# Silu gates in pairs with the attention outputs multiplied in, sums of x by need, squares moved, and two gate tiles ahead of the stick-breaking stage

## The chip, the cores and the metric

The kernel runs on one core of a Trainium2 chip. The metric is the device time of one execution in microseconds (us); the time of a kernel is the median of its runs. The profile is one further execution, recorded by the hardware profiler; its time and its span stand in the table below.

## What is computed

One decoder layer with two attention branches that read the same normalised input, over 16 meta tokens and 2048 real tokens, width 1024, all in float32:

```python
xn = rms_norm(h, norm_gain)                 # h = [pad, 16 meta tokens, x]
proj = xn @ w_in                            # 6400 columns, split into:
sb_q, sb_k, sb_v, sw_q, sw_k, sw_v, sb_z, sw_z, g_sb, g_sw = split(proj)
o_sb = stick_breaking_attention(sb_q, sb_k, sb_v)       # 8 heads of 64, all earlier tokens
o_sw = sliding_window_sink_attention(rope(sw_q), rope(sw_k), sw_v)   # 16 heads, window 128
y_sb = (o_sb * silu(sb_z)) @ w_branch_sb
y_sw = (o_sw * silu(sw_z)) @ w_branch_swa
merged = sigmoid(g_sb) * y_sb + sigmoid(g_sw) * y_sw
out = rms_norm(h + merged @ w_out, final_norm_gain)
```

A stick-breaking weight is exp(log_sigmoid(z) + the sum over the later keys of log_sigmoid(-z)). The change concerns the gates: `sb_z` (4 column tiles of 128, called SBZ), `sw_z` (8, SWZ), `g_sb` (8, GSB) and `g_sw` (8, GSW), 28 column tiles of `proj` in all.

## The kernel before

**Tiling.** The tokens lie in reverse in 4 groups of 512. A column tile is 128 columns of `w_in` for one group: the product of a 1024 x 128 weight tile with the group's 1024 x 512 normalised x. Each float32 operand is split into a high and a low part (`xh`, `xl`; `wh`, `wl`), and a product is high by high, high by low and low by high: 3 matmuls of 128x128 by 128x512 for each of 8 slices of 128, so 24 to a column tile (lines 412 to 414). The splitting of a raw weight is a cast on ScalarE (ACT) and a subtraction on VectorE (DVE), or both on GpSimd in some stages; the split weights are written to DRAM (`h_in_w_in`, `l_in_w_in`) the first time, and loaded from there in the second half.

**Stages.** The groups are done in two halves, [2, 3] and then [0, 1]. A half has a sliding-window stage, then a stick-breaking stage (function `stick`), into which gate column tiles are woven so that TensorE (PE) has work while the scans of the stick run on DVE, then the gate **pairs**, then two last gate tiles. After half 0 stands `prep`, which normalises the x of the next half (its row sums of squares are needed for that). After half 1 stands `finish`, the two branch projections, the merge and the output projection. One gate tile (`gts[1:2]`) stands alone ahead of each stick stage; `REST` (12 and 18) says how many gate tiles are done before the pairs; two single column tiles open the pairs stage.

**A pair** is two gate column tiles for both groups of the half, done with seven half-size products in place of eight (functions `pair_weights`, `seven`, `gate_pair`): sums and differences of the weights (`s`, `s4`), made on DVE, meet sums and differences of x (`t1` to `t4`), made once per half by `sums_of_x`. A product is 12 matmuls. PE takes them in the order 11·11, s2·t2, 12·21, s1·t1, s3·t3, 22·t4, then the next pair's 11·11, then s4·22. The first pair comes while `t1` to `t4` are still being made. For each k of 4, `sums_of_x` makes x11, x12, x22 whole (line 598), then differences (609 to 611), the splits of t2, t3, t1 (603, 604), then t4 (616).

**Squares.** The sums of squares for the next half's x are made inside the stick stage of half 0: 16 tiles `xq` are loaded (in a ring of two, shared with the tiles `q2` of the stick's queries) and squared on ACT with an accumulated sum (line 1004). The reciprocal root stands between the stick stage and the pairs.

**Gated outputs.** Silu gates are written to DRAM (`zs`, `zw`), attention outputs too (`od` of the stick, `ow` of the window). `gated` (line 197) later loads a tile of each, multiplies them on DVE (line 202) and splits the product (204, 206) for the branch projections: `od, zs` inside `finish`, `ow, zw` beside the last two gate tiles.

**What sets the order.** PE's order is that of the code, by hand (`manual_schedule`). The other engines' order is made by a scheduler, and each engine runs its list in order. All DMAs are issued by SyncE (SP) through one helper (lines 55 to 58), in order: a DMA that waits holds those behind it. Buffers are rings: `xs` (4 buffers, function `ring_x`), `tmp` (7), `wh` and `wl` (3 each), `raw` (2).

## Time and profile before

| | before |
|---|---|
| time, median of 3 runs | 2176.36 us (2169.45 to 2180.69) |
| the profiled execution: time, span | 2171.38 us, 2169.7 us |
| granted TensorE clock, mean of the span | 0.988 |
| PE busy | 2106.6 us (97%) |
| DVE, ACT, GpSimd busy | 1497.0 (69%), 1072.5 (49%), 246.9 us (11%) |
| DMA | 389.82 MB, 180 GB/s over the span |
| PE idle for a load of the stick's queries (`q<-qd`) | 8.5 us in 2 waits |
| ACT idle for the tiles `xq` | 20.6 us in 11 waits |
| loads of `gated`: `tmp<-ow`, `tmp<-zw` beside the last tiles; `a<-od`, `a<-zs`, `a<-ow`, `a<-zw` in `finish` | 16 of 256 KB each |

The stages in the span (us): stick of half 0 from about 375 to 610, pairs of half 0 from 610, the last gate tiles and `prep` around 780, the second half's stick from 1140 to 1620, its pairs from 1620, the last tiles with `gated` from about 1700, then `finish`. PE is busy nearly throughout, so what a change can win is PE's idle stretches and the lower clock that follows them. A window of the profile lists, for a stretch, each engine's busy time with its count of instructions, the clock granted to PE (1.00 is full) and the DMA engines' busy share.

### The profile page before, as it was taken

To read this page: it belongs to the slowest core of one execution; us is meant where nothing else is said; L and a number is where in the kernel's file an instruction comes from. 1 tells how busy PE (TensorE), PEld (TensorE's weight loads), DVE (VectorE), ACT (ScalarE), POOL (GpSimd) and SP (SyncE) were. 2 spreads that over 40 slices of the span, in tenths; PEclk is the share of its full clock that TensorE was granted. 3 is DMA by queue.
4 is the path that set the end of the run, shared out by engine and by line. 5 is a ranking of instruction groups with operands and counts; after the bars stand their busy time and mean duration, and the time that the engine had idled before them with its cause. 6 is when DMAs were issued, how large, how long until landed. Compare 5 with 4: busy or idle time off the path is not lost.

```text
span 2169.7 us, 29865 instructions
## 1 busy us (share of the span) xinstructions
PE 2106.6 (97%) x10426; PEld 1744.1 (80%) x10426; DVE 1497.0 (69%) x2350; ACT 1072.5 (49%) x2541; POOL 246.9 (11%) x303
## 2 busy tenths in 40 slices
PE   8999999999989999999989999999999899999998
PEld 6788887778868878888878888888887688887887
DVE  7897885777785543877748888888884455554453
ACT  6677774556653234777745666666651211321131
POOL 2122334112000100122210000000000132000000
PEclk9999999999999999999999999999999899999999
DMA  9855546756436864544364333344235895558432
GB/s 335 302 175 176 193 146 203 227 177 199 163 112 222 297 215 157 164 154 148 136 195 124 110 122 117 117 120 124 72 106 197 302 356 184 196 200 299 148 118 78
DMA packets 178838, 389.82 MB, mean 180 GB/s; under 512 B 23200, under 2 KB 41440, under 8 KB 178688
## 3 DMA queue, kind: packets, MB, share of 16 engines
q1 hardware_dynamic: 178688, 387.92, 52.9%
q8 instruction: 82, 1.34, 0.3%
q14 instruction: 68, 0.56, 0.1%
HBM read 242.07 MB, written 145.70 MB: 179 GB/s over the span
## 4 chain that ended last, share of the span: by engine, by line
PE 79%; DVE 9%; DMA 6%; ACT 3%; issue 2%; SPq 1%; DVEq 0%; ACTq 0%
PE ps_g L412 10%; PE ps_g L413 10%; PE ps_g L414 10%; PE ps_z L1020 5%; PE ps_o L1076 5%; PE ps_t L1045 5%; PE ps_o L907 2%; PE ps_z L861 2%; PE ps_t L674 2%; PE ps_g L674 2%; PE ps_z L674 2%; DMA xq<-in_x 1%; PE ps_z L234 1%; PE ps_z L235 1%; PE ps_z L236 1%
## 5 line engine op out<-in xcount | busy, mean ns | idle before, releaser
L412 PE MATMUL ps_g<-xh,wh 128*128 128x512 f32 x1224 | 505.0, 413 | 10.0 <-ACT xh L1128 7.0
L413 PE MATMUL ps_g<-xl,wh 128*128 128x512 f32 x1224 | 482.6, 394 | 0.2
L414 PE MATMUL ps_g<-xh,wl 128*128 128x512 f32 x1224 | 481.9, 394 | 0.0
L414 PEld LDWEIGHTS ps_g<-xh,wl 128*128 128x128 f32 x1224 | 231.3, 189 | 52.3 <-DVE wl L112 0.4
L412 PEld LDWEIGHTS ps_g<-xh,wh 128*128 128x128 f32 x1224 | 232.4, 190 | 47.7 <-ACT xh L1128 7.0
L413 PEld LDWEIGHTS ps_g<-xl,wh 128*128 128x128 f32 x1224 | 232.7, 190 | 37.2 <-DVE xl L1129 1.3
L1023 ACT ACTIVATE row<-ps_z 128x512 f32<-128x512 f32 (+2 forms) x320 | 165.3, 516 | 141.9 <-PE ps_z L1020 129.3
L1032 DVE TENSOR_TENSOR_SCAN row<-row 128x528 f32<-128x528 f32 (+1 forms) x192 | 216.0, 1126 | 26.8 <-ACT row L1023 22.9
L116 DVE SCALAR_TENSOR_TENSOR wtl<-ps_t,wth 128x512 fp32r<-128x512 f32 (+1 forms) x320 | 189.7, 593 | 26.2 <-ACT wth L115 25.3
L1030 DVE TENSOR_TENSOR_SCAN row<-row,mask 128x512 f32<-128x512 f32 (+4 forms) x128 | 147.5, 1153 | 67.5 <-ACT row L1023 66.4
L115 ACT ACTIVATE wth<-ps_t 128x512 fp32r<-128x512 f32 (+1 forms) x320 | 170.5, 533 | 47.4 <-PE ps_t L1045 45.7
L1020 PE MATMUL ps_z<-kt,q 128*128 128x512 f32 (+4 forms) x640 | 181.4, 359 | 8.5 <-DMA q<-qd 8.5
L1045 PE MATMUL ps_t<-ident,row 128*128 128x128 f32 x1088 | 171.9, 273 | 8.6 <-DVE wtl L116 4.5
L1045 PEld LDWEIGHTS ps_t<-ident,row 128*128 128x128 f32 x1088 | 134.3, 140 | 44.8 <-DVE wtl L116 8.5
L111 POOL TENSOR_SCALAR wh<-raw 128x1024 fp32r<-128x1024 f32 (+1 forms) x49 | 52.3, 1067 | 1016.0 <-PE ps_o L674 558.8
L1020 PEld LDWEIGHTS ps_z<-kt,q 128*128 128x128 f32 x640 | 118.1, 190 | 30.6 <-issue 9.5
L1076 PE MATMUL ps_o<-wth,vc 128*128 128x512 f32 (+1 forms) x320 | 129.9, 406 | 1.7 <-ACT tmp L1080 1.7
L869 ACT ACTIVATE sc<-sc,nm 128x129 f32<-128x129 f32 x256 | 100.0, 393 | 40.9 <-DVE nm L867 40.1
L1076 PE MATMUL ps_o<-wtl,vc 128*128 128x512 f32 (+1 forms) x320 | 116.9, 365 | 0.2
L273 ACT CAST ringl<-gt 128x512 fp32r<-128x512 f32 x32 | 19.9, 622 | 137.2 <-DVE gt L271 134.4
L861 PEld LDWEIGHTS ps_z<-kk,q 128*128 128x128 f32 x512 | 69.7, 190 | 6.6 <-DVE q L842 0.7
L299 ACT ACTIVATE sq<-res 128x512 bf16<-128x512 f32 x32 | 20.2, 632 | 108.8 <-DVE res L295 108.7
(398 smaller groups left out, 4182.7 us busy)
## 6 DMA issues: line engine op xcount, KB each, us to landing
wh<-h_in_w_in SPq DMA_DIRECT2D x60, 512.0 KB
wl<-l_in_w_in SPq DMA_DIRECT2D x60, 512.0 KB
raw<-in_w_in SPq DMA_DIRECT2D x50, 512.0 KB
h_in_w_in<-wh SPq DMA_DIRECT2D x41, 512.0 KB
l_in_w_in<-wl SPq DMA_DIRECT2D x41, 512.0 KB
q<-qd SPq DMA_DIRECT2D x128, 128.0 KB
vc<-vd SPq DMA_DIRECT2D x48, 256.0 KB
kd<-tmp SPq DMA_DIRECT2D x32, 256.0 KB
```

Of the source, the lines that this page charges most:

```text
L115: A.activation(h, acc, AF.Copy, scale=scale)
L116: V.scalar_tensor_tensor(l, acc, scale, f32(h), op0=ALU.mult, op1=ALU.subtract)
L412: T.matmul(acc, lhsT=wh[:, k, :], rhs=xh[g][:, k, :], start=k == 0, stop=False)
L413: T.matmul(acc, lhsT=wh[:, k, :], rhs=xl[g][:, k, :], start=False, stop=False)
L414: T.matmul(acc, lhsT=wl[:, k, :], rhs=xh[g][:, k, :], start=False, stop=k == KT - 1)
L674: T.matmul(acc, lhsT=l[:, k, :], rhs=r[:, k, :], start=first and k == i == 0, stop=k == KT // 2 - 1 and i == 2, skip_group_check=not (firs ...
L1020: T.matmul(acc[:, :b - a], lhsT=lq, rhs=kt[h][:, k0 + a:k0 + b], start=t == 0, stop=t == 1)
L1023: A.activation(r[:, a:b], acc[:, :b - a], AF.Sigmoid, scale=-1.0)
L1030: V.tensor_tensor_scan(r[:, :w], r[:, :w], mask[0][:, :w], 1.0, op0=ALU.mult, op1=ALU.max)
L1032: V.tensor_tensor_scan(r[:, :w], r[:, :w], r[:, :w], last[j], op0=ALU.mult, op1=ALU.min)
L1045: T.transpose(tr[:, j * P:(j + 1) * P], rows_of[h, g, n - (j > i), j][:, k0:k0 + P], ident)
L1076: T.matmul(o[:, :n], lhsT=v, rhs=r, start=first and r is wh, stop=last and r is wl)
```

## The change

1. **Order of the gates.** There is now one order per half. Half 0 has 14 plain sigmoid gates first (GSB 0 to 7, GSW 0 to 5), then the 12 silu gates (SWZ 0 to 7, SBZ 0 to 3) as its six pairs, then the last two GSW. Half 1 has 12 plain ones, SWZ 0 to 5, two plain ones, and three pairs of SWZ 6, 7 and SBZ 0 to 3.
2. **Outputs multiplied in the pairs of half 0.** There each silu gate's tile is multiplied by its attention output (`times`: a load of `ow` or `od` into an `xs` buffer and a DVE multiplication, line 730 of the changed kernel). `gated` then loads one tile and multiplies nothing for the groups of half 0 (its second argument is `None`); for half 1 it is as before.
3. **Sums of x by need.** `sums_of_x` makes t2, t1 and t3 for all k, holding t1 in PSUM banks and t3 in the four `xs` buffers, then splits t1 and t3, then makes t4 from x21 less both parts of t2 (13 DVE instructions a k where there were 12). In the first pair (`lead`) the product 12·21 comes right after 11·11 in a bank of its own, and one DVE addition joins them.
4. **Squares among the pairs.** The 16 loads of x and Squares for the next half leave the stick stage and stand, four each, behind pairs 0 to 3 of half 0, in `xs` buffers; the reciprocal root stands behind pair 4.
5. **Two gate tiles ahead** of each stick stage instead of one (`gts[1:3]`), so one fewer is woven in.
6. **End of half 0.** The scale rows are made right after the pairs; both last tiles of group 2 come before `prep` and both of group 3 after it (before, one of group 3 stood ahead of it).

The number of PE matmuls for gates and pairs is the same. The diff, with repeated context left out:

```diff
         for k, g in keys:
-            a, b = stg(), stg()
+            a = stg()
             DMA(a, src[k][g])
-            DMA(b, zz[k][g])
-            V.tensor_tensor(a, a, b, op=ALU.mult)
+            if zz is not None:
+                b = stg()
+                DMA(b, zz[k][g])
+                V.tensor_tensor(a, a, b, op=ALU.mult)
...
-                    osb = gated(od, zs, [(k, g) for g in groups for k in range(4)], lambda: ringr(1), lambda: small("a", AB))
+                    osb = gated(*((zs, None) if half == 0 else (od, zs)), [(k, g) for g in groups for k in range(4)], lambda: ringr(1), lambda: small("a", AB))
...
-        for k in range(KT // 2):
-            yield q
+        ks = range(KT // 2)
+        held = [], []
+        for k in ks:
             b11, b12, b22 = (whole(n, k) for n in ("11", "12", "22"))
-            V.tensor_tensor(b11, b12, b11, op=ALU.subtract)
-            V.tensor_tensor(b12, b22, b12, op=ALU.subtract)
-            V.tensor_tensor(b22, b22, b11, op=ALU.subtract)
-            halves_of("t2", k, b22)
-            halves_of("t3", k, b12)
-            halves_of("t1", k, b11)
-            b21 = whole("21", k)
-            V.tensor_tensor(b21, b21, b22, op=ALU.subtract)
-            halves_of("t4", k, b21)
+            t3, t1 = ring_x(), ps(("t", "t", "o", "zm")[k])
+            V.tensor_tensor(t3, b22, b12, op=ALU.subtract)
+            V.tensor_tensor(b22, t3, b11, op=ALU.add)
+            parted("t2", k, b22)
+            V.tensor_tensor(t1, b12, b11, op=ALU.subtract)
+            held[0].append(t1)
+            held[1].append(t3)
+        yield q
+        for n, ts in zip(("t1", "t3"), held):
+            for k in ks:
+                parted(n, k, ts[k])
+        for k in ks:
+            b21, (t2h, t2l) = whole("21", k), (f32(t[:, k, :]) for t in q["t2"])
+            V.tensor_tensor(b21, b21, t2h, op=ALU.subtract)
+            V.tensor_tensor(b21, b21, t2l, op=ALU.subtract)
+            parted("t4", k, b21)
         yield q
...
-        product(a0, "11", "11", True, False)
+        product(a0, "11", "11", True, lead)
         A.copy(p1, a0)
+        if lead:
+            a3 = ps(tag)
+            product(a3, "12", "21", True, True)
+            t = tmp()
+            V.tensor_tensor(t, a3, p1, op=ALU.add)
+            use(0, 0, t)
         yield
...
-        product(a0, "12", "21", False, True)
-        use(0, 0, a0)
+        if not lead:
+            product(a0, "12", "21", False, True)
+            use(0, 0, a0)
+        a3 = ps(tag)
...
             if silu:
                 V.tensor_tensor(e, t, e, op=ALU.mult)
+            if times:
+                o = ring_x()
+                DMA(o, src[groups[n]])
+                V.tensor_tensor(e, e, o, op=ALU.mult)
             DMA(dst[groups[n]], e)
...
-                for g1, ssq in list(sums_of.items())[n1 // 8:n1 // 8 + 1]:
-                    i, f = divmod(n1 % 8, 2)
-                    t = bp.tile([P, GT], F32, tag="q2", name="xq", bufs=2)
-                    DMA(t, x[g1 * GT + i * P:g1 * GT + (i + 1) * P, f * GT:(f + 1) * GT])
-                    A.activation(t, t, AF.Square, accum_out=ssq[:, f, i:i + 1])
...
+    gss = ([*plain[:14], *silu, *plain[14:]], [*plain[:12], *silu[:6], *plain[12:14], *silu[6:], *plain[14:]])
...
-            drain(tiles_by_tile(gts[1:2], groups))
+            drain(tiles_by_tile(gts[1:3], groups))
...
+            for n in todo:
+                if half == 0:
+                    for g, i, f in squared[4 * n:4 * n + 4]:
+                        t = ring_x()
+                        DMA(t, x[g * GT + i * P:g * GT + (i + 1) * P, f * GT:(f + 1) * GT])
+                        A.activation(t, t, AF.Square, accum_out=next_sums[g][:, f, i:i + 1])
+                if half == 0 and n == 4:
...
+                    rsqrt(rs, t, tp, t=u)
...
         if half == 0:
+            rb = scale_rows(rs0)
             ts = [mk() for mk in gts[26:]]
-            drain(by_group(ts, groups[:1]), by_group(ts[:1], groups[1:]))
-            prep(halves[1][0], rs0)
-            drain(by_group(ts[1:], groups[1:]))
+            drain(by_group(ts, groups[:1]))
+            prep(halves[1][0], rs0, rb)
+            drain(by_group(ts, groups[1:]))
...
-                osw.update(gated(ow, zw, todo[:6], ringl, tmp))
+                osw.update(gated(zw, None, todo[:6], ringl, tmp))
```

What the scheduler makes of it stands in the lists of the engines. ACT, at the end of the first pair of half 0, where the weights of the second pair are cast; before (`wh_7587`, `wh_7589`, `wh_7591` are the second pair's casts):

```order
L636 CAST wh_7587<-raw_7595 128x1024
L705 ACTIVATE tmp_7541<-ps_g_7496 128x512
L636 CAST tmp_7603<-raw_7597 128x512
L705 ACTIVATE tmp_7497<-tmp_7497 128x512
L705 ACTIVATE tmp_7515<-tmp_7515 128x512
L636 CAST wh_7589<-s_7599 128x1024
L636 CAST wh_7591<-raw_7597 128x1024
L636 CAST s4h_7593<-tmp_7600 128x512
```

and now (L1367 is the Square, L724 the sigmoid, `wh_7550` and `wh_7552` are the second pair's casts for s2, s3 and for s1, 22):

```order
L1367 ACTIVATE xs_7623,ssq_7438<-xs_7623 128x512
L1367 ACTIVATE xs_7626,ssq_7438<-xs_7626 128x512
L724 ACTIVATE tmp_7534<-tmp_7441 128x512
L1367 ACTIVATE xs_7629,ssq_7438<-xs_7629 128x512
L724 ACTIVATE tmp_7541<-tmp_7480 128x512
L647 CAST tmp_7564<-raw_7558 128x512
L1367 ACTIVATE xs_7632,ssq_7438<-xs_7632 128x512
L647 CAST wh_7550<-s_7560 128x1024
L647 CAST wh_7552<-raw_7558 128x1024
```

The four Squares of the first pair now stand ahead of the second pair's two large casts, where only sigmoids stood. SP at the same place, before (`raw` is a raw weight tile coming in, `gw2_2` the gate tile 2 of group 2 going out):

```order
L58 DMA raw_7597<-in_w_in 128x1024
L58 DMA h_in_w_in_5888_7617<-wh_7587 128x1024
L58 DMA gw2_2_217<-tmp_7541 128x512
L58 DMA l_in_w_in_5888_7618<-wl_7588 128x1024
L58 DMA h_in_w_in_6016_7619<-tmp_7603 128x512
L58 DMA l_in_w_in_6016_7620<-tmp_7604 128x512
L58 DMA gw3_3_222<-tmp_7497 128x512
L58 DMA gw3_2_221<-tmp_7515 128x512
L58 DMA raw_7741<-in_w_in 128x1024
```

and now:

```order
L58 DMA xs_7623<-in_x 128x512
L58 DMA xs_7626<-in_x 128x512
L58 DMA xs_7629<-in_x 128x512
L58 DMA xs_7632<-in_x 128x512
L58 DMA zw1_3_150<-tmp_7534 128x512
L58 DMA xs_7667<-ow2_2_265 128x512
L58 DMA h_in_w_in_3712_7580<-tmp_7564 128x512
L58 DMA l_in_w_in_3712_7581<-tmp_7565 128x512
L58 DMA xs_7714<-ow3_3_270 128x512
L58 DMA zw1_2_149<-tmp_7541 128x512
L58 DMA xs_7721<-ow3_2_269 128x512
L58 DMA raw_7733<-in_w_in 128x1024
```

Four loads of x, right behind the store of the pair's first output (`zw0_2`), now stand ahead of the other outputs' stores and of the third pair's raw weights (`raw_7733`), and the second, third and fourth of them each wait for the Square of the one ahead, because they take the same one of the four `xs` buffers in turn; the other three still hold attention outputs for that pair. DVE at the start of the pairs stage of half 0, before:

```order
L609 TENSOR_TENSOR tmp<-tmp 128x512
L611 TENSOR_TENSOR tmp<-tmp 128x512
L604 TENSOR_TENSOR t3l<-tmp,t3h 128x512
L610 TENSOR_TENSOR tmp<-tmp 128x512
L616 TENSOR_TENSOR tmp<-tmp 128x512
L598 TENSOR_TENSOR tmp<-xh,xl 128x512
L604 TENSOR_TENSOR t1l<-tmp,t1h 128x512
L604 TENSOR_TENSOR t2l<-tmp,t2h 128x512
```

and now, the same place:

```order
L617 TENSOR_TENSOR ps_t<-tmp 128x512
L614 TENSOR_TENSOR xs<-tmp 128x512
L617 TENSOR_TENSOR ps_t<-tmp 128x512
L1101 TENSOR_TENSOR xs<-tmp,xs 128x512
L601 TENSOR_TENSOR tmp<-xh,xl 128x512
L615 TENSOR_TENSOR tmp<-xs,tmp 128x512
```

and further down, behind the splits of the first pair's weights:

```order
L648 TENSOR_TENSOR wl<-raw,wh 128x1024
L627 TENSOR_TENSOR tmp<-tmp,t2l 128x512 x4
L726 TENSOR_TENSOR tmp<-tmp 128x512
L653 TENSOR_TENSOR s<-raw 128x512
L607 TENSOR_TENSOR t4l<-tmp,t4h 128x512 x3
L730 TENSOR_TENSOR tmp<-tmp,xs 128x512
```

All of t4's work (616 and 604 before, now 626, 627 and 607) has moved behind the other three sums and behind the splits of the first pair's weights, and the first multiplication by an attention output (730) stands behind nearly all of it.

More of the change, by code (lines that the diff above doesn't have):

```diff
@@ L666, in pair_weights, with seven @@
                 "s3": (t3h[:, hi], t3l[:, hi]), "s1": (t2h[:, lo], t2l[:, lo]), "22": (t2h[:, hi], t2l[:, hi]), "s4": t4}
-    def seven(w, b, tag, use):
+    def seven(w, b, tag, use, lead):
         def product(acc, n, m, first, last):
@@ L697, in seven, with gate_pair @@
         use(0, 1, u2)
-    def gate_pair(bp, ga, gb, groups, q, tag, plain):
+    def gate_pair(bp, ga, gb, groups, q, tag, plain, lead, times):
         tiles = ga, gb
         def use(m, n, t):
-            c0, dst, silu = tiles[m]
-            e = tmp() if silu or t.dtype != F32 or n == m == 0 else t
+            c0, dst, silu, src = tiles[m]
+            e = tmp()
             A.activation(e, t, AF.Sigmoid)
@@ L710, in gate_pair @@
         yield
-        yield from seven(w, q, tag, use)
+        yield from seven(w, q, tag, use, lead)
     def in_line(pairs):
@@ L717, in in_line @@
                 next(g)
[L718 removed]
+                yield n
                 next(g)
@@ L940, in window, with stick @@
         return sw_k, sw_v, sw_q, attend, ending
-    def stick(groups, bp, sums_of={}):
+    def stick(groups, bp):
         kt, vc = {}, {}
@@ L1109, in tile_kernel @@
                                               (sb_k, 2), (sb_v, 2), (sb_q, 2), (sb_k, 3), (sb_v, 3), (sb_q, 3))]
[L1110 to L1113 removed]
+    plain = ([(C_GSB + p * P, gs[p], False, None) for p in range(8)] + [(C_GSW + p * P, gw[p], False, None) for p in range(8)])
+    silu = ([(C_SWZ + p * P, zw[p], True, ow[p]) for p in range(8)] + [(C_SBZ + p * P, zs[p], True, od[p]) for p in range(4)])
+    gss = ([*plain[:14], *silu, *plain[14:]], [*plain[:12], *silu[:6], *plain[12:14], *silu[6:], *plain[14:]])
+    gts_of = [[lambda s=s: gate(*s[:3]) for s in order] for order in gss]
     halves = ([2, 3], [0, 1])
@@ L1276, in tile_kernel @@
     for half, groups in enumerate(halves):
+        gts = gts_of[half]
         with tc.tile_pool(name=f"swa{half}", bufs=1, side="left") as sp:
@@ L1319, in tile_kernel @@
             vsplit[0] = False
-            next_sums = {g: sums() for g in halves[1]} if half == 0 else {}
-            side = stick(groups, bp, next_sums)
-            drain(tiles_by_tile(gts[1:2], groups))
+            side = stick(groups, bp)
+            drain(tiles_by_tile(gts[1:3], groups))
             rest = REST[half]
             cost_sb = 8 * sum(4 * (4 - g) for g in groups) * 1.31 + 8 * 0.75
-            ratio = cost_sb / ((rest - 2) * 10.4)
-            weave(tiles_by_tile(gts[2:rest], groups), side, ratio)
+            ratio = cost_sb / ((rest - 3) * 10.4)
+            weave(tiles_by_tile(gts[3:rest], groups), side, ratio)
             drain(side)
-            if half == 0:
-                t, u = (bp.tile([P, GT], F32, tag="wh", name="sum", bufs=3)[:, :8] for _ in range(2))
-                for n, ssq in enumerate(next_sums.values()):
-                    V.tensor_tensor(t[:, 4 * n:4 * n + 4], ssq[:, 0], ssq[:, 1], op=ALU.add)
-                rs = tp.tile([P, 8], F32, tag="rs8", name="rs", bufs=1)
-                rsqrt(rs, t, tp, t=u)
-                rs0, rs1 = rs[:, :4], rs[:, 4:]
         with tc.tile_pool(name=f"pairs{half}", bufs=1, side="left") as bp:
@@ L1339, in tile_kernel @@
             sums_q = sums_of_x(bp, groups)
-            tq = [next(sums_q) for _ in range(3)][0]
+            tq = next(sums_q)
             for n, (w, use, _) in enumerate(ts):
```

33 lines of the change are left out of this document (17 added, 16 removed).

## The prediction

> **What bounds the kernel now.** I read the page's busy shares first, then PE's waits, then a table of windows, to see where PE loses time.
>
> ```profile
> PE 2106.6 (97%) x10426; PEld 1744.1 (80%) x10426; DVE 1497.0 (69%) x2350; ACT 1072.5 (49%) x2541; POOL 246.9 (11%) x303
> ```
>
> PE is the bound. The change leaves its matmuls' number as it is, so only three things can move the end: PE's idle time, the lower clock behind an idle stretch, and stalls that the change adds. PE's waits (us in total, times, longest):
>
> ```profile
> PE ps_z L1020 <- DMA q<-qd: 8.5, 2, 5.7
> PE ps_z L674 <- ACT t2h L603: 6.4, 2, 5.0
> PE ps_g L235 <- DVE ringl L206: 5.1, 4, 2.2
> PE ps_t L1045 <- DVE wtl L116: 4.5, 7, 1.5
> PE ps_z L674 <- ACT wh L636: 4.1, 1, 4.1
> PE ps_t L1045 <- DVE wm L116: 3.9, 3, 2.1
> PE ps_g L234 <- ACT ringl L204: 3.9, 1, 3.9
> PE ps_g L412 <- ACT xh L386: 2.7, 1, 2.7
> ```
>
> The change touches each of these. The windows (busy us of PE, PEld, DVE, ACT, POOL, then PE's clock, the DMA engines' busy share and GB/s) place them:
>
> ```profile
> 350.00:375.00 25.00, 23.00 (x105) 18.54 (x103) 8.42 (x16) 7.22 (x11) 10.80 (x12) 1.00 0.65 213
> 375.00:400.00 25.00, 24.20 (x120) 20.09 (x120) 18.41 (x22) 13.01 (x38) 4.43 (x3) 0.93 0.79 247
> 400.00:610.00 210.00, 200.28 (x1101) 166.04 (x1100) 157.84 (x212) 127.15 (x330) 25.58 (x16) 1.00 0.56 182
> 625.00:650.00 25.00, 16.81 (x60) 12.22 (x59) 24.93 (x40) 11.68 (x19) 0.00 (x0) 0.85 0.36 127
> 675.00:700.00 25.00, 25.00 (x112) 20.71 (x111) 15.51 (x21) 8.50 (x12) 0.00 (x0) 1.00 0.62 230
> 775.00:800.00 25.00, 22.16 (x87) 16.99 (x86) 17.27 (x26) 11.58 (x20) 0.00 (x0) 0.86 0.73 240
> 1125.00:1150.00 25.00, 19.25 (x78) 15.29 (x77) 9.34 (x10) 6.25 (x11) 0.83 (x2) 0.86 0.97 282
> 1150.00:1620.00 470.00, 469.31 (x2569) 393.84 (x2568) 410.20 (x504) 283.95 (x600) 0.00 (x0) 1.00 0.35 109
> 1625.00:1650.00 25.00, 19.67 (x78) 15.35 (x77) 15.07 (x24) 6.39 (x12) 0.00 (x0) 0.86 0.45 152
> 1700.00:1725.00 25.00, 18.41 (x71) 13.39 (x69) 10.02 (x15) 7.21 (x11) 7.20 (x4) 0.85 0.91 336
> 1725.00:1750.00 25.00, 24.42 (x97) 19.75 (x97) 15.83 (x23) 5.58 (x9) 3.46 (x2) 0.87 0.78 262
> ```
>
> The loss of a window is at most its idle time plus (1 - clock) x 25 us; the second part counts idle time at the low clock twice, so I go somewhat below it in the sum. Stick of half 0 loses 9.7 us idle in 210, that of half 1 only 0.7 in 470. The opening of the pairs of half 0 (625 to 650) loses 8.2 + 3.75 = 11.9, with DVE busy for 24.93 of 25.
>
> **Part by part.**
>
> *Squares out of the stick (part 4, the gain).* ACT waits for the loads of these tiles while the stick's casts stand behind them:
>
> ```profile
> ACT xq L1004 <- DMA xq<-in_x: 20.6, 11, 3.6
> L58 SPq DMA_DIRECT2D xq<-in_x x16: 332/537/1057, 372.2 to 579.8; - x16
> L1004 ACT ACTIVATE xq<-xq x16: 621/632/635, 377.4 to 582.3; 128x512 f32<-128x512 f32 x16
> L1004 ACT ACTIVATION_READ_ACCUMULATOR xq<-xq x16: 183/186/200, 377.9 to 582.9; 128x1 f32 x16
> ```
>
> Half 1's stick has no such loads and no such idle time, though DVE is at 410.2 of 470 (87%) there against 157.8 of 210 (75%) here. So I give these 9.7 us back but for the 0.7: **-9**. Bounds: -4, if the waits for wtl and wm (4.5 + 3.9) are DVE's own; -13, if the pace beside them improves too.
>
> *The same Squares among the pairs (part 4, the cost).* In the first pair the loads form a chain, since each waits for the Square ahead of it, and ACT runs its list in order, so the second pair's casts wait for the fourth Square. Here are PE's matmuls at the first pair, then DVE around them:
>
> ```profile
> 632.27 0.39 PE L674 MATMUL ps_g<-xh,wh 128*128 128x512 f32 x1
> ...
> 634.77 0.39 PE L674 MATMUL ps_g<-xh,wl 128*128 128x512 f32 x1
> 639.28 0.79 PE L674 MATMUL ps_z<-t2h,wh 128*128 128x512 f32 x1 [4.12 <-ACT wh L636]
> ...
> 642.47 0.79 PE L674 MATMUL ps_z<-t2h,wl 128*128 128x512 f32 x1 [1.98 <-DVE wl L637]
> ...
> 647.26 0.50 PE L674 MATMUL ps_z<-t2h,wh 128*128 128x512 f32 x1 [1.44 <-ACT t2h L603]
> 648.42 0.51 PE L674 MATMUL ps_z<-t2l,wh 128*128 128x512 f32 x1 [0.66 <-DVE t2l L604]
> ```
>
> ```profile
> 612.45 0.17 DVE L126 TENSOR_TENSOR sum<-rs 128x8 f32<-128x8 f32 x1 [2.35 <-ACT rs L122]
> ...
> 645.27 0.68 DVE L604 TENSOR_TENSOR t1l<-tmp,t1h 128x512 fp32r<-128x512 f32 x1
> 645.88 0.68 DVE L611 TENSOR_TENSOR tmp<-tmp 128x512 f32<-128x512 f32 x1
> 649.49 0.68 DVE L683 TENSOR_TENSOR tmp<-ps_z,tmp 128x512 f32<-128x512 f32 x1
> ```
>
> Twelve matmuls start within 2.50 us, so one takes 0.227, a product of 12 takes 2.72 and a pair of seven 19.04. DVE starts a 128x512 instruction every 0.61. The sums can start about 2.4 us earlier than before, since the root's wait is gone (2.35), but DVE has more ahead of the first output's multiplication: four more additions for t4 (2.4), one for the lead product, two silu multiplications (together 1.8), and the next pair's 1.2 us split. From 649.5: 649.5 - 2.4 + 2.4 + 1.8 + 1.2 = 652.5. SP issues the first x load then.
>
> One link is a load and its Square. From issue to Square took 5.2 us for the first tile (372.2 to 377.4) and 2.5 for the last (579.8 to 582.3); Square and accumulator read are 0.82. I take 3.2 + 0.8 = 4.0, nearer to the last because SP holds everything else back during the chain; bounds 3.5 and 6.2. Four links end at 668.5; the cast and the split of the weights follow:
>
> ```profile
> L636 ACT CAST wh<-s 128x1024 fp32r<-128x1024 f32 x6 | 6.3, 1049 | 14.0 <-PE ps_z L674 11.7 <-DVE s L644 2.2
> L637 DVE TENSOR_TENSOR wl<-s,wh 128x1024 fp32r<-128x1024 f32 x6 | 7.3, 1219 | 0.9 <-ACT wh L636 0.9
> ```
>
> That is 668.5 + 1.05 + 1.2 = 670.7. PE needs them for the second pair's s2·t2, eight products after 632.3, plus the stalls that I leave in the opening (next paragraph, 6.9): 632.3 + 21.8 + 6.9 = 661.0. It idles 9.7, and the clock costs up to another 3.75 (0.85 in the windows with such a stall): **+13.5**. In the second pair the third and fourth load are not chained to each other. Its first output is ready some 11 us after PE restarts (two products, slowed, then sigmoid and multiplications); three links, a Square, cast and split make 11 + 12 + 0.8 + 2.3 = 26. PE comes to the third pair's s2·t2 after 19.04 + 3.75 = 22.8: 3.3 idle and 2.7 of clock, **+6**. In the third and fourth pair the casts stand ahead of most Squares: 0.
>
> A price from the Trainium skill, "SBUF — State Buffer", section "The DMA setup-cost knee": a transfer costs about 2 us plus its bytes over 436 GB/s, an estimate of 2.6 us for 256 KB. Both xq rows bracket it; by it a link is 3.4, the first stall 2.4 us shorter and the second 1.8, and the sum would be 4 lower.
>
> *Opening of the pairs (parts 3 and 1's order).* Before, PE waited 6.1 for weights, whose splits stood behind the sums on DVE, and 2.1 for t2. Now t2 comes first and PE has 12·21 (2.72) to do before it needs s2's weights, but about 41 DVE instructions (41 x 0.61 = 25 from 610.5) still end at 635.5, then come cast (1.05) and, behind three more DVE instructions (1.8), the split (1.2): 639.5 against 632.3 + 5.4 = 637.7, nearly 2 idle. t4, needed by the sixth product at 632.3 + 13.6 + 2 = 648, ends with DVE at about 652.5 in four pieces: some 3.4 idle. With 1.5 of clock 6.9 are left of 11.9: **-5**; bounds -12 (all gone) and 0.
>
> *Two tiles ahead of each stick (part 5).* PE waits 8.5 us for queries whose loads are queued at 0.97 DMA share. A gate tile for two groups is 48 matmuls x 0.227 = 10.9 us of cover, more than the 5.7 of the longer wait. Half 0 (350 to 400, at most 2.8 + 1.75): **-4** (0 to -4.5). Half 1 (at most 5.75 + 3.5): **-7** (-3 to -9).
>
> *Half 1's stick* now has silu gates in it, 6 tiles x 2 groups against 4 x 2 ones: at most 12 more DVE multiplications of 0.7, on a DVE busy 87% of the time: **+1** (0 to +6).
>
> *Sums in half 1* (1625, at most 5.3 + 3.5): t2 first removes the 5.0 us wait; t4 comes late there too: **-6** (-2 to -8).
>
> *Gated outputs of half 0 (part 2).* 32 loads of 256 KB run beside the last tiles at 336 GB/s and 0.91 DMA share, where PE waits for ringl (5.1 + 3.9). 16 of them and 16 multiplications go. The two windows lose 6.6 + 3.75 + 0.6 + 3.25 at most, 14.2: **-10** (-5 to -12). What replaces them, 24 loads and multiplications in the pairs of half 0, lies beside DVE at 15.5 of 25 and DMA at 0.62: 0, if that cover holds (third rival).
>
> *End of half 0 (part 6).* PE's 2.7 for xh is a wait on a load of x behind other SP issues; the scale rows come earlier, but SP still waits for PE ahead of the last load: **-1** (-6 to +2).
>
> Sum: -9 + 13.5 + 6 - 5 - 4 - 7 + 1 - 6 - 10 - 1 = **-21.5** on the profiled execution's 2171.4 (span 2169.7 and 1.7 around it), so 2150. The median of the runs lies 5.0 above that execution, so against it **2155 us**.
>
> The clock's rule in the Trainium skill ("TensorE: Matmul & The Clock Gate", Part 1) says that a re-warming takes about 3.4 us at half rate, which would cost an estimated 1.7 us a stall. The windows' 0.85 stands for up to 3.75, idle included, so the trace costs more; by the rule the two new stalls were 3 us cheaper and the removed ones 1 to 2 each, which nearly cancels.
>
> **The rivals.**
>
> 1. *The chain costs nothing* (the loads overlap or end sooner than PE comes): 13.5 and 6 fall out: 2155 - 19.5 = 2135. For it: in the pairs as they were PE has no idle time from 675 on. Against: each load waits for a Square by name, and ACT did wait 20.6 us for the same loads.
> 2. *The chain runs at the slowest row.* With links of 6.2 the first stall is 4 x 2.2 = 8.8 longer, the second 3 x 2.2 = 6.6: 2155 + 15.4 = 2170, no change that can be told. For it: the pairs add 1 MB of x and 1 MB of outputs each 19 us. Near it (2164) lies the case that the stick's stalls stay (9 not won).
> 3. *Slower: DMA becomes the bound of the pairs of half 0.* Now 230 GB/s at share 0.62; 2 MB more per 19.04 us are 110 GB/s, so 340, which is what stalls PE at 1700 (336 GB/s, 0.91). If then the first stall costs 22.3, the second 12.6 (as in 2) and pairs three and four 14 each like the first in my sum: 2155 + 15.4 + 28 = 2198. It decides from a loss of over 32 us in those pairs beyond my sum. Against: raw stores and loads drop out of the path while SP is held, and the later casts stand ahead of their Squares.
>
> **How the numbers follow.** Forecast 0.53, rival 1 0.17, rival 2 with its neighbour 0.20, rival 3 0.10. A measurement of this kernel tells 0.5% (about 11 us) from no change: faster is under 2165.5, slower over 2187. Rival 1 and nearly all of the forecast are faster, and the 2164 case barely: 0.17 + 0.48 + 0.04 = 0.69. Slower is rival 3, 0.10; the rest, 0.21, is the same. The forecast's own range is 2144 to 2166 (links 3.5 to 5, and the other terms' halves); with rival 1's centre and rival 2 the range is 2134 to 2176.
>
> **What would show it.** Right: PE idle before the second pair's s2·t2 for an ACT cast, about 10 us, while ACT waits for x loads at the Squares (some 12 us in the first pair), and a shorter one in the third pair; no `q<-qd` wait at either stick; PE over 205 of 210 us busy in half 0's stick; no t2h wait; under 4 us for ringl. Wrong: no idle time before the second pair (rival 1), PE idle in the third and fourth pair as well (rival 3), or half 0's stick still waiting for wtl and wm. The forecast fails as a whole if the pairs of half 0 lose more than 32 us beyond it.

## The result and the profile after

| | before | changed |
|---|---|---|
| median | 2174.44 us (4 runs, 2169.45 to 2180.69) | 2149.89 us (4 runs, 2146.81 to 2152.05) |
| profiled execution, span | 2171.38, 2169.7 us | 2152.05, 2150.3 us |

The changed kernel is faster: ratio 0.9885, 95% interval 0.9855 to 0.9914, so 19 to 32 us of 2174. Predicted were 2155 (2134 to 2176). Between the two profiled executions lie 19.3 us, between the medians 24.6; the changed kernel's profiled execution is the slowest of its four runs. PE remains the bound, with the same 10426 matmuls; the first line of the page, and PE's waits over the whole span of the changed kernel (us in total, times, longest):

```profile
PE 2097.5 (98%) x10426; PEld 1740.7 (81%) x10426; DVE 1503.4 (70%) x2360; ACT 1070.5 (50%) x2541; POOL 244.1 (11%) x303
```

```profile
PE ps_z L685 <- ACT wh L647: 10.0, 2, 7.8
...
PE ps_z L685 <- DVE tmp L700: 6.7, 2, 5.7
PE ps_t L1063 <- DVE wtl L116: 6.1, 8, 1.5
PE ps_z L685 <- DVE wl L648: 2.8, 2, 2.2
...
PE ps_g L237 <- DVE ringl L208: 1.4, 1, 1.4
PE ps_o L1094 <- DMA q<-qd: 1.3, 1, 1.3
```

Gone or nearly gone are the 8.5 us for queries, the 6.4 for t2h and most of the 9.0 for ringl. New are 10.0 us for weights of pairs (L647) and 6.7 for a DVE addition (L700); the 6.1 for wtl are more than the 4.5 before. Where in the span, by the windows (busy us of PE, PEld, DVE, ACT, POOL, then clock, DMA share, GB/s):

```profile
350.00:375.00 25.00, 25.00 (x115) 20.52 (x114) 5.29 (x11) 6.88 (x11) 11.12 (x12) 1.00 0.67 211
375.00:400.00 25.00, 24.66 (x125) 20.56 (x124) 13.78 (x16) 10.37 (x28) 3.86 (x3) 1.00 0.84 276
400.00:610.00 210.00, 202.05 (x1118) 168.40 (x1117) 171.72 (x222) 124.58 (x311) 25.88 (x18) 1.00 0.49 157
625.00:650.00 25.00, 17.12 (x59) 13.28 (x58) 21.13 (x33) 9.45 (x15) 0.00 (x0) 0.80 0.50 170
650.00:675.00 25.00, 22.22 (x96) 17.66 (x96) 16.93 (x24) 8.80 (x16) 0.00 (x0) 1.00 0.69 240
675.00:700.00 25.00, 17.13 (x64) 13.15 (x63) 12.72 (x18) 9.38 (x18) 0.00 (x0) 0.80 0.63 212
1125.00:1150.00 25.00, 25.00 (x111) 20.65 (x110) 2.36 (x5) 3.70 (x7) 2.10 (x4) 1.00 0.73 212
1150.00:1610.00 460.00, 458.75 (x2523) 384.51 (x2522) 409.42 (x501) 281.63 (x602) 0.00 (x0) 1.00 0.36 113
1625.00:1650.00 25.00, 24.00 (x106) 19.56 (x105) 17.32 (x28) 6.86 (x12) 0.00 (x0) 1.00 0.60 210
1700.00:1725.00 25.00, 25.00 (x112) 20.64 (x111) 9.70 (x14) 10.02 (x16) 3.46 (x2) 1.00 0.84 293
```

In four places PE hardly idles now: the starts of both sticks (350 to 400, 1125 to 1150), the sums of half 1 (1625) and the last gate tiles (1700). Two places pay: the opening of half 0's pairs, at 625, loses as much as before (7.9 us idle, clock 0.80), and a new stall lies at 675 (7.9 idle, clock 0.80), with a small one ahead of it (2.8, in the window at 650). And one that should have won did not: the stick of half 0 (400 to 610) is idle for 7.95 us, after 9.7.

The chain stands in ACT's timeline (start, duration, [idle time ahead, what ended it]), first pair and second pair:

```profile
648.70 0.63 ACT L1367 ACTIVATE xs<-xs 128x512 f32<-128x512 f32 x1 [6.64 <-DMA xs<-in_x]
...
652.13 0.63 ACT L1367 ACTIVATE xs<-xs 128x512 f32<-128x512 f32 x1 [2.70 <-DMA xs<-in_x]
...
655.46 0.63 ACT L1367 ACTIVATE xs<-xs 128x512 f32<-128x512 f32 x1 [2.09 <-DMA xs<-in_x]
...
659.15 0.63 ACT L1367 ACTIVATE xs<-xs 128x512 f32<-128x512 f32 x1 [1.94 <-DMA xs<-in_x]
...
660.05 1.04 ACT L647 CAST wh<-s 128x1024 fp32r<-128x1024 f32 x1 [0.17 <-DVE s L655]
...
678.23 0.63 ACT L1367 ACTIVATE xs<-xs 128x512 f32<-128x512 f32 x1 [8.99 <-issue]
...
687.52 0.63 ACT L1367 ACTIVATE xs<-xs 128x512 f32<-128x512 f32 x1 [1.53 <-DMA xs<-in_x]
...
688.15 1.03 ACT L647 CAST wh<-s 128x1024 fp32r<-128x1024 f32 x1
```

In both pairs the cast for the next pair's s2 (L647) starts right behind the fourth Square. In the first pair it waits 0.17 us more, for DVE's sum `s` (L655), which is late for the same reason: DVE's multiplications had waited for the sigmoids that stand between the Squares. PE at the same places:

```profile
645.68 0.79 PE L685 MATMUL ps_z<-t3h,wh 128*128 128x512 f32 x1 [5.65 <-DVE tmp L700]
...
661.15 0.50 PE L685 MATMUL ps_z<-t2h,wh 128*128 128x512 f32 x1 [2.19 <-ACT wh L647]
...
689.23 0.79 PE L685 MATMUL ps_z<-t2h,wh 128*128 128x512 f32 x1 [7.83 <-ACT wh L647]
```

The second pair's s2·t2 waits 2.2 us (and 0.6 more for `wl`), the third pair's 7.8. The first row is a wait that the prediction did not have: the product s3·t3 adds into the bank of s2·t2, which DVE must have read first (line 700), and that addition stands on DVE behind t4's work and the first output's multiplication:

```profile
642.54 1.88 DVE L607 TENSOR_TENSOR t4l<-tmp,t4h 128x512 fp32r<-128x512 f32 x3
644.35 0.68 DVE L730 TENSOR_TENSOR tmp<-tmp,xs 128x512 f32<-128x512 f32 x1
644.95 0.68 DVE L700 TENSOR_TENSOR tmp<-ps_z,tmp 128x512 f32<-128x512 f32 x1
```

### The profile page after: what moved, and what is told of

Its sections match the earlier page's. It is cut to its first block, busy times and chain, and to the rows that moved or that the text cites. A ratio compares the mean times of both kernels' runs of the same rounds, so it can differ in the third digit from the quotient of the medians.

```text
span 2150.3 us, 29875 instructions
## 1 busy us (share of the span) xinstructions
PE 2097.5 (98%) x10426; PEld 1740.7 (81%) x10426; DVE 1503.4 (70%) x2360; ACT 1070.5 (50%) x2541; POOL 244.1 (11%) x303
## 4 chain that ended last, share of the span: by engine, by line
PE 63%; DVE 3%; ACT 1%; issue 1%; DMA 0%; DVEq 0%; SPq 0%; ACTq 0%
PE ps_g L415 7%; PE ps_g L416 7%; PE ps_g L417 7%; PE ps_o L1094 4%; PE ps_z L1038 4%; PE ps_t L1063 4%; PE ps_z L685 2%; PE ps_t L685 1%; PE ps_g L237 1%; PE ps_g L238 1%; PE ps_g L236 1%; PE ps_z L238 1%; PE ps_z L237 1%; PE ps_z L236 1%; PE ps_z L885 1%; PE ps_t L238 1%
## 5 line engine op out<-in xcount | busy, mean ns | idle before, releaser
L116 DVE SCALAR_TENSOR_TENSOR wtl<-ps_t,wth 128x512 fp32r<-128x512 f32 (+1 forms) x320 | 189.5, 592 | 18.0 <-ACT wth L115 17.1
L1038 PEld LDWEIGHTS ps_z<-kt,q 128*128 128x128 f32 x640 | 117.4, 188 | 22.1 <-ACT row L1041 0.8
L583 ACT ACTIVATE tmp<-ps_g 128x512 f32<-128x512 f32 x72 | 43.0, 598 | 76.0 <-PE ps_g L417 63.5
```

What stands on the lines that cost most here:

```text
L116: V.scalar_tensor_tensor(l, acc, scale, f32(h), op0=ALU.mult, op1=ALU.subtract)
L1038: T.matmul(acc[:, :b - a], lhsT=lq, rhs=kt[h][:, k0 + a:k0 + b], start=t == 0, stop=t == 1)
```

## The experiments

Ratios are to the kernel before, run beside each. Times can be set against each other within e1, e2, e7 and e4, within e8, e6, e9 and e10, and within e11, e12 and e13, since each of these sets ran on one chip beside the same runs of the kernel before. Across the sets, and against the changed kernel (0.9885, 0.9855 to 0.9914), the ratios are compared.

**e1: Squares back in the stick.** Of the changed kernel, part 4 undone:

```diff
+                    t = bp.tile([P, GT], F32, tag="q2", name="xq", bufs=2)     # in stick, as before
+                    DMA(t, x[...])
+                    A.activation(t, t, AF.Square, accum_out=ssq[:, f, i:i + 1])
...
-                        t = ring_x()                                           # among the pairs
-                        DMA(t, x[...])
-                        A.activation(t, t, AF.Square, accum_out=next_sums[g][:, f, i:i + 1])
```

> The changed kernel with part 4 undone: the 16 loads of x and Squares are back in the stick stage of half 0, the reciprocal root stays behind the fifth pair. The chain theory (Squares in the pairs hold the next pair's casts) expects PE's waits before the second and third pair's s2·t2 (2.2 + 0.6 and 7.8 us, with their clock some 13 us) to go. With it two cases for the stick: if the xq loads stall PE there as the prediction's -9 had it, those 9 come back and the time is about 2146 us (ratio to before 0.987); if the stick's stalls are DVE's own, nothing comes back and it is about 2138 us (ratio 0.983). A theory that the waits in the pairs come from something else (DMA load, DVE) expects 2150 to 2160.

Measured: 2147.64 us, ratio 0.9877 (0.9862 to 0.9893), the case in which the stick takes back what the pairs give. PE's waits for casts in the pairs (L647) are down to 1.0 us, from 10.0, and the stick of half 0 (400 to 610) is idle for 14.7 us at clock 0.98, after 7.95 at 1.00.

**e2: the kernel before without any Squares:**

```diff
-                    t = bp.tile([P, GT], F32, tag="q2", name="xq", bufs=2)
-                    DMA(t, x[...])
-                    A.activation(t, t, AF.Square, accum_out=ssq[:, f, i:i + 1])
+                    G.memset(ssq[:, f, i:i + 1], 512.0)
```

> The kernel before with the 16 loads of x and Squares of the stick stage left out (a constant stands for the sums of squares, so half 1 is normalised by a wrong scale). The prediction's term (these loads cost PE 9 us in the stick) expects about 2165 us, ratio 0.996, with PE's waits for wtl, wm and tmp in the stick of half 0 down from 9.5 to under 2 us. The rival (those waits are DVE's own, since after has 7.6 us of them without any xq) expects 2172 to 2174, ratio 0.998 to 1, and at least 7 us of the waits left.

Measured: 2161.78 us, ratio 0.9943 (0.9930 to 0.9956). **e7: the changed kernel without any Squares** (the same edit there):

> The changed kernel with the 16 loads of x and Squares left out altogether (a constant in their place, so half 1 is normalised by a wrong scale). The chain theory expects the waits at the second and third pair to go, about 13 us with their clock: 2137 us, ratio 0.983, while the opening of the pairs keeps its waits (2.2 for wl, 5.7 for a DVE addition). If the second pair's wait only moves (DVE or weights late anyway), over 2142.

Measured: 2135.50 us, ratio 0.9827 (0.9814 to 0.9839). The Squares cost 11.8 us in the stick of the kernel before (2173.59 to e2), 12.1 in the stick of the changed one (e1 to e7), and about as much among the pairs (0.9885 to 0.9827 is 0.0058, some 13 us, of which the changed kernel's interval leaves 6 to either side open). So moving them won nothing that the intervals can tell: 12 us left the stick and some 13 came back. By the windows they came back in two places: between 605 and 720 the changed kernel is idle for 18.5 us and e7 for 11.8, and between 750 and 800, at the end of half 0, for 4.4 us and not at all; the lower clock behind these stretches comes on top. Without Squares the stick of half 0 is idle for 3.5 us of 210 in the kernel before, and for 7.6 of 200 in the changed one, which has none in its stick either; these rows are of e2 and of e7:

```profile
400.00:610.00 210.00, 206.52 (x1136) 173.21 (x1135) 167.42 (x225) 124.62 (x305) 27.05 (x18) 1.00 0.51 167
```

```profile
400.00:600.00 200.00, 192.45 (x1073) 160.77 (x1072) 161.40 (x208) 118.57 (x301) 23.75 (x15) 1.00 0.49 159
```

Something else in the change costs the stick some 4 us idle; e8 asks for it. In e7 the new waits for casts in the pairs are down to 1.0 us in all, while the wait for line 700 (8.4 in all) is still there.

**e4: Squares two pairs later.**

```diff
-                if half == 0:
-                    for g, i, f in squared[4 * n:4 * n + 4]:
+                if half == 0 and n > 1:
+                    for g, i, f in squared[4 * n - 8:4 * n - 4]:
...
-                if half == 0 and n == 4:
+                if half == 0 and n == 5:
```

> The changed kernel with the Squares two pairs later (four each behind the third to the sixth pair, the root behind the sixth). If what costs is only that Squares stand ahead of the casts at the first two pairs, about 2138 us, ratio 0.983, with no PE wait between the third and the last pair. If loads of x cost in any pair (DMA is at 0.96 to 0.99 in the third and fourth pair already), the waits reappear at later pairs or at the end of half 0, where the root and the scale rows now come later: 2143 to 2155.

Measured: 2157.56 us, ratio 0.9931 (0.9919 to 0.9942): slower than the changed kernel, but not in the pairs. There PE waited no more behind the opening than without Squares (1.2 us in each of the windows at 650 and 675, as in e7), though the DMA engines were full. The loss against e7, 22.1 us, is one wait at the end of half 0, for the root that the scale rows need:

```profile
700.00:725.00 25.00, 25.00 (x112) 20.72 (x111) 19.86 (x30) 11.18 (x21) 0.00 (x0) 1.00 1.02 390
```

```profile
PE ps_t L373 <- DVE rs L129: 21.9, 1, 21.9
```

So the x loads do not stall PE by their traffic; a Square stalls it where a cast or the root stands behind it. **e9: the same, with the root in two parts** (the second group's only where its x is normalised):

```diff
...                                            # root(n): the root of group n's sums; in the next half:
-                rs = rs1
+                rs = root(1)
...                                            # Squares as in e4
                 if half == 0 and n == 4:
-                    ...                        # root of both groups
+                    rs0 = root(0)
```

> The changed kernel with the Squares two pairs later, as in e4, but with the reciprocal root in two parts: that of the first group of the next half behind the fifth pair, that of the second group only where its x is normalised, in the next half. So the 21.9 us wait of e4 should go without the chain of the first two pairs coming back. If nothing else is late: as without Squares, 2136 to 2140, ratio 0.983 to 0.985. If the last eight loads, which stand before those of the last gate tiles and of the normalisation on SP, hold those up: 2142 to 2150.

Measured: 2148.72 us, ratio 0.9891 (0.9877 to 0.9906). The wait fell from 21.9 to 8.8 us, now for the second group's root, whose last Squares ran at 779 and 781 us, behind the pairs' outputs on SP. In the pairs PE waited no more than in e4. The last eight Squares came too late for it.

**e8: part 5 alone on the kernel before.**

```diff
-            drain(tiles_by_tile(gts[1:2], groups))
+            drain(tiles_by_tile(gts[1:3], groups))
...
-            ratio = cost_sb / ((rest - 2) * 10.4)
-            weave(tiles_by_tile(gts[2:rest], groups), side, ratio)
+            ratio = cost_sb / ((rest - 3) * 10.4)
+            weave(tiles_by_tile(gts[3:rest], groups), side, ratio)
```

> The kernel before with part 5 alone: two gate tiles ahead of each stick stage. The prediction's terms (-4 and -7) expect 2162, ratio 0.995, with no q<-qd wait at either stick. The rival, from the stick of half 0 in the changed kernel (7.6 us of PE waits without any xq where before without Squares has 3.8), is that one fewer woven tile costs the stick of half 0 some 4 to 8 us: then 2167 to 2170, ratio 0.997 to 0.999.

Measured: 2167.29 us against 2172.77, ratio 0.9979 (0.9969 to 0.9989): 5.5 us (2 to 7 by the interval), half of the 11 of the prediction. Both waits for queries are gone, but the stick of half 0 is idle for 15.4 us of 210 at clock 0.98, where it was 9.7 at 1.00:

```profile
400.00:610.00 210.00, 194.64 (x1056) 160.32 (x1055) 161.16 (x207) 126.64 (x334) 24.83 (x15) 0.98 0.53 172
```

```profile
PE ps_t L1045 <- DVE wtl L116: 8.2, 10, 1.5
...
PE ps_t L1045 <- DVE wm L116: 5.3, 5, 2.5
...
PE ps_o L1076 <- ACT tmp L1080: 3.0, 3, 1.7
```

These were 4.5, 3.9 and 1.7. A tile that stands ahead of the stick is missing in the weave, and PE reaches the stick's own steps sooner than DVE and ACT have them. (The profiled execution, 2170.56 us, lies 3.3 above e8's median, so a typical run may lose somewhat less there.) In half 1 the windows show no such cost: from 1150 to 1610 PE is idle for 1.0 us, after 0.7, and the 5.75 us at 1125 are gone.

**e6: part 2 undone** (outputs of half 0 multiplied late, as before):

```diff
-                    osb = gated(*((zs, None) if half == 0 else (od, zs)), ...
+                    osb = gated(od, zs, ...
...
-                                      half == 0 and n < PLAIN, n == rest + 2, half == 0) ...
+                                      half == 0 and n < PLAIN, n == rest + 2, False) ...
...
-                osw.update(gated(zw, None, todo[:6], ringl, tmp))
+                osw.update(gated(ow, zw, todo[:6], ringl, tmp))
```

> The changed kernel with part 2 undone: the pairs of half 0 store the silu gates alone, and the outputs of half 0 are loaded and multiplied beside the last gate tiles and in the finish, as before. The prediction's term (-10) expects the ringl waits back at the last gate tiles (about 10 us with their clock) and the pairs of half 0 as they were: 2160, ratio 0.993. If the 24 loads and multiplications in the pairs of half 0 cost something too (their loads hold the xs buffers that force the Squares' chain), the pairs win back part of it: with free xs buffers the chain may go (13 us): 2147 to 2152.

Measured: 2148.70 us, ratio 0.9890 (0.9875 to 0.9905), the same as the changed kernel. The windows of e6 show both sides:

```profile
675.00:700.00 25.00, 23.82 (x105) 19.10 (x104) 19.12 (x27) 10.69 (x15) 0.00 (x0) 1.00 0.67 241
1675.00:1700.00 25.00, 17.73 (x75) 13.26 (x73) 9.25 (x13) 6.99 (x11) 7.20 (x4) 0.98 0.90 341
```

The last gate tiles lose 7.3 us idle again, and the stall at 675 is gone (1.2 us idle, clock 1.00, in place of 7.9 at 0.80). In e6 no output loads hold `xs` buffers, so the loads of x run ahead: on ACT the first six Squares stand ahead of the first pair's large casts (631.1), and all sixteen are done by 647.4, ahead of the second pair's (658.8). ACT waits for x for 4.3 us in all, against 21.9 in the changed kernel. So the chain is a product of parts 2 and 4 together: with outputs in three of the four `xs` buffers, the loads of x pass through the fourth.

**e10: part 3 undone** (sums in the old order, no lead product: `sums_of_x` and the first pair as before).

> The changed kernel with part 3 undone: sums of x in the old order and no lead product. The prediction's terms (-5 at the opening of half 0's pairs, -6 at half 1's) expect 2161, ratio 0.994. From the changed kernel's trace, whose opening of half 0 loses as much as before (11.9 us in 625 to 650, now mostly for a DVE addition that stands behind t4's work), only half 1's 6 come back and the chain's stalls may shift: 2154 to 2157.

Measured: 2154.78 us, ratio 0.9920 (0.9906 to 0.9934). By the ratios part 3 is worth some 8 us (0.0035 of 2173), not 11, and the two intervals overlap, so even that is not certain. The traces don't place it: between 605 and 720 PE waits 17.1 us with the old order (12.6 of it for casts of weights) and 18.5 with the new; at half 1's pairs it waits 2.4 for t2 with the old order (5.4 in the kernel before, with the same order) and 1.0 for line 700 with the new. So of the 5.4 in half 1 about 3 went for another reason than the order of the sums; which one stays open.

**e11: Squares in the stick with a ring of their own, loads issued one step ahead.**

```diff
+        def fetch():
+            if len(fetched) < len(squares):
+                t = bp.tile([P, GT], F32, tag="xq", name="xq", bufs=3)
+                DMA(t, squares[len(fetched)][0])
+                fetched.append(t)
...                                            # at the first step of each head and group
+                n1 = len(state) - 1
+                for _ in range(2 if n1 == 0 else 1):
+                    fetch()
+                if n1 < len(squares):
+                    t = fetched[n1]
+                    A.activation(t, t, AF.Square, accum_out=squares[n1][1])
```

> The changed kernel with the 16 loads of x and Squares back in the stick stage of half 0, but in a ring of three buffers of their own, each load issued one head and group (some 14 us) ahead of its Square. In e1, with the loads in the queries' ring and right ahead of their Squares, they cost 12 us there (e1 against e7). If that cost is ACT waiting for a load with the stick's casts behind it, it goes, and the time comes near that without any Squares: 2136 to 2139, ratio 0.983 to 0.985, with no ACT wait for xq. If it is the Squares' time on ACT (16 x 0.8) or their loads' traffic, 2143 to 2148 as in e1.

Measured: 2139.82 us, ratio 0.9863 (0.9841 to 0.9884). Of the Squares' 12 us, how much is left is not certain: 2.5 us by the profiled executions (2137.78, and e7's 2135.32), 4 by the medians, 8 by the ratios, and e11's interval reaches into e1's. The windows speak for a small rest: from 350 to 600 PE is idle for 14.9 us in e1, 10.2 in e11 and 7.9 in e7. But the gain did not come in the way expected. The Squares of e1 are spread over the stick; those of e11 are not (first and last start in each row, e1 then e11):

```profile
L1028 ACT ACTIVATE xq<-xq x16: 627/632/633, 378.9 to 590.3; 128x512 f32<-128x512 f32 x16
```

```profile
L1035 ACT ACTIVATE xq<-xq x16: 620/632/654, 376.9 to 426.5; 128x512 f32<-128x512 f32 x16
```

With its own ring the scheduler took all sixteen within the first 50 us. The loads did not run 14 us ahead: the first was issued at 372.2 and the last at 423.0, 4.7 and 3.5 us ahead of their Squares. ACT still waited 13.2 us for them, 11.2 of it ahead of 410, where the stick has only begun. The ring and the earlier loads were not tried apart.

**e12: e11 with one tile ahead of half 0's stick** (`gts[1:2 + half]`).

> e11 with one gate tile ahead of the stick of half 0 again (half 1 keeps two). By e8, where two tiles ahead of both sticks gained 5.5 us of the 12.6 that the windows at the sticks' starts lost, the second tile ahead of half 0 is worth nothing or costs: the wait for queries comes back (about 5 us in 350 to 400) and the stick's own waits fall by 4 to 7: e11 -3 to +1. If one fewer woven tile costs the stick nothing once the xq loads are out of the way: e11 + 4 to + 6.

Measured: 2135.53 us, ratio 0.9833 (0.9819 to 0.9848); e11 less 4.3, though the two intervals overlap a little. The stick's idle time (400 to 600) falls from 8.0 to 4.2 us of 200, and at its start (350 to 400) it rises from 2.2 to 4.4 of 50.

**e13: e11 with s3·t3 of the first pair in a bank of its own.**

```diff
-        product(a1, "s3", "t3", False, True)
-        V.tensor_tensor(u3, a1, p1, op=ALU.add)
+        if lead:
+            a4 = ps({"o": "zm", "zm": "o"}[tag])
+            product(a4, "s3", "t3", True, True)
+            V.tensor_tensor(u3, a4, u2, op=ALU.add)
+        else:
+            product(a1, "s3", "t3", False, True)
+            V.tensor_tensor(u3, a1, p1, op=ALU.add)
```

> e11 with the first pair's s3·t3 in a PSUM bank of its own, so that PE needn't wait until DVE has read s2·t2 (line 700, which stands behind t4's work on DVE; 5.7 us of PE's idle time in the changed kernel at half 0's opening, 1.0 at half 1's). If the reading is right, that wait goes and a smaller one for t4 takes its place two products later: e11 - 2 to - 5. If DVE's amount of work at the opening is the bound, the same idle time only shows at 22·t4: e11 - 1 to + 1.

Measured: 2136.70 us, ratio 0.9839 (0.9824 to 0.9853). No wait for line 700 is left; what stands in its place at the pairs' openings is smaller:

```profile
PE ps_z L685 <- ACT wh L647: 3.0, 2, 2.5
...
PE ps_zm L685 <- DVE t4l L607: 1.0, 2, 0.6
```

Between 600 and 800 PE is idle for 9.0 us, after 13.3 in e11. By itself the gain of 3.1 us over e11 is inside the two intervals.

**e14: e12 and e13 together.**

> e12 (Squares in the stick with prefetched loads, one tile ahead of half 0's stick, two ahead of half 1's) with the first pair's s3·t3 in a bank of its own, as in e13. If the two gains add (e12 under e11 by 4.3, e13 under e11 by 3.1), about 2132, ratio 0.982. If e11's median was high by chance and the wait at the opening only moves, e12 again: 2135 to 2137.

Measured: 2130.43 us, ratio 0.9803 (0.9790 to 0.9816), the fastest kernel here, 42 us under the kernel before and, by the ratios, 18 under the changed one. Its interval lies wholly under e12's, so the bank of its own is worth about 5 to 7 us (0.0030 of 2173 by the ratios). Against e13, e14 differs by the one tile ahead of half 0's stick alone, and the two intervals lie apart: 0.0036 of 2173, some 8 us, 6.3 by the medians. So in half 0 the second tile costs more than it covers; by e8's windows it pays in half 1. The first row is e13's, the others are e14's:

```profile
400.00:600.00 200.00, 190.93 (x1057) 159.64 (x1056) 159.62 (x205) 121.99 (x317) 22.70 (x14) 0.99 0.53 171
400.00:600.00 200.00, 196.68 (x1089) 165.23 (x1088) 156.66 (x203) 122.72 (x317) 27.34 (x16) 1.00 0.55 180
625.00:650.00 25.00, 21.87 (x87) 16.94 (x86) 24.89 (x39) 10.36 (x16) 0.00 (x0) 0.93 0.58 198
650.00:675.00 25.00, 22.45 (x92) 17.68 (x91) 17.97 (x27) 8.43 (x13) 0.00 (x0) 0.93 0.63 213
675.00:700.00 25.00, 23.82 (x104) 19.10 (x104) 21.48 (x31) 9.72 (x14) 0.00 (x0) 1.00 0.84 297
```

With the start of the stick (350 to 600) the idle time falls from 10.8 us in e13 to 6.7 in e14.

## Why the prediction was right, and where it was not

The predicted sum, -21.5 us on the profiled execution, met 19.3 between the two profiles, but partly by luck. The two tiles won 5.5 us in place of 11 and the opening of half 0's pairs nothing in place of 5; the chain cost 13 in place of 19.5, and the Squares gave 11.8 in the stick in place of 9. These errors nearly cancel. The 5.0 that was then added for the median was a mistake of small samples: with more runs the median of before was 2171.5 to 2174.4, not 2176.4.

- **Squares out of the stick, -9: right, a little small.** e2 measured 11.8, and PE's idle time in that stick fell from 9.7 to 3.5.
- **Two tiles ahead, -4 and -7: both waits went, but the step that gave the second tile no price failed.** The cover of 10.9 us ahead of the stick is taken from the weave inside it. e8 gives 5.5 in place of 11, and e13 against e14 shows that in half 0 the tile costs more than it covers. That is why the stick of half 0 shows 7.95 us idle in the changed kernel although its Squares are gone: the two terms met there. So a sign named for being right failed (202.05 us busy, not over 205 of 210), and one named for being wrong came true in part: PE still waits for `wtl`, 6.1 us over the span after 4.5, though only 0.4 for `wm` after 3.9. The cause is the tile, not the Squares.
- **The chain, +13.5 and +6: right in mechanism and place, too high by half, and wrong in the shares.** The four Squares start 3.43, 3.33 and 3.69 us apart; 4.0 had been taken. Counted from the pairs' start (which came 7 us earlier), the chain ended when predicted: the fourth Square ended at 659.9, 35.0 us behind the first pair's first matmul (624.9), where 36.2 had been worked out. But PE came later than predicted, because the opening lost more and so hid part of the chain; the first stall was 2.8 us in place of 9.7, and the clock stayed at 1.00 behind it. In the second pair the first load was issued at 673.8, 12.7 us after PE restarted (11 had been taken), and its Square began 4.4 later, a link of 5.2 with the Square. PE was there after 20.3 us, not 22.8, since no low clock had followed the first stall; so the second stall was 7.8 in place of 3.3. e7 puts the Squares' whole cost behind the stick at some 13 us, and part of that, the 4.4 us idle at the end of half 0, lies where the prediction had counted nothing for them.
- The Trainium skill's transfer price ("SBUF — State Buffer", "The DMA setup-cost knee", about 2 us plus bytes over 436 GB/s, an estimate of 2.6 us for 256 KB and 3.4 for a link) agrees with the links of 3.3 to 3.7 better than the 4.0 taken from the xq rows.
- **The opening of half 0's pairs, -5: failed.** It lost 7.9 us idle at clock 0.80, about as before (8.2 at 0.85). The two times that it worked out were nearly right: PE's wait for s2's weights was 2.2 us (nearly 2), and DVE ended t4 at 646.2, 21.3 us behind the first matmul (20.2). What the step left out is line 700, which stands on DVE behind most of t4's work and which PE needs before it may add s3·t3 into the same bank, one product ahead of the place where the prediction has PE wait. e13 and e14 removed that wait; in e14 the window at 625 is idle for 3.1 us.
- **Half 1's sums, -6: the size was right, the cause only in part.** The window at 1625 has 1.0 us idle at full clock, after 5.3 at 0.86; but e10, with the old order, waits only 2.4 for t2 there.
- **Gated outputs, -10: right where it was counted, wrong in what it was said to cost.** The window at 1700 has no idle time. But "0, if that cover holds" for the loads in the pairs named DVE and DMA as the cover; what they took was the `xs` buffers. e6 shows the net of part 2, with part 4 beside it, to be nothing.
- **Half 1's stick, +1:** 458.75 of 460 us busy, so 1.3 idle after 0.7. **End of half 0, -1:** between 750 and 800 PE is idle for 4.4 us, in place of 2.8 at a lower clock, so nothing was won. In e1, e6 and e7, where no late Squares stand in the pairs, PE is busy there for 50.00 of 50; the loss goes with the late Squares, not with part 6.
- **The rivals.** The free chain fell by the traces. That e7, without Squares, ran 2135.50 and the rival's number was 2135 is chance: the rival took 19.5 us off, and e7 some 13. A bound by DMA in the pairs fell by the changed kernel itself, where PE is busy for 50.00 of 50 from 700 to 750 at shares of 0.96 and 0.99, and by e4: share 1.02, PE busy for 25.00 of 25.

## What to carry to other kernels

An activation that reads a freshly loaded buffer holds back everything behind it on an engine that runs in order, so count who takes the buffers of its ring: loads that were independent in the code became a chain because other loads held three of four buffers. Work put ahead of a stage as cover is work that the stage's own weave then lacks; price both places. A product that adds into a bank which another engine must read first makes PE wait for all that stands ahead of that read in the engine's list; a bank of its own took that wait away here. A small side computation that needs only its own data is worth a ring of its own: here three buffers and earlier loads left 2.5 to 8 us of a cost of 12, while moving the work to another stage won nothing that the intervals can tell.
